# A rebuilt opening: x read feature by token, its squares summed on TensorE, and the gate sums moved out of the dense stream

## The chip, the cores and the metric

The kernel runs on one core of one Trainium2 chip. The metric is device microseconds (us) of one execution; the median of three runs is quoted, and one further execution was taken with the hardware profiler.

## The reference, cut to what matters

One step of a one-layer decoder trunk. There are 1024 prompt tokens and 64 sample tokens (8 sequences of 8), 1088 in all, with 1024 features each. All of it is float32.

```python
shift, scale, gate = jnp.split(jax.nn.silu(c) @ ada_w[l] + ada_b[l], 3, axis=-1)
h = rmsnorm(x, norm_w[l]) * (1.0 + scale[:, None, :]) + shift[:, None, :]
q_lat, kv_lat, k_pe, g_a, u, g_b, m_a, m_b = split_in(h @ w_in[l])   # 4128 columns
...                                   # attention, convolution and recurrence, two output products
x = x + gate[:, None, :] * (merged @ w_out[l])
```

`rmsnorm` divides each token's row by the root of its mean square. The condition `c` has one row for the prompt and one for each of the 8 sample sequences, so `shift`, `scale` and `gate` have 9 rows of 1024.

## The kernel before, in words

**Layout.** Activations stand with features on the 128 partitions and tokens along the free axis, in 8 blocks of features (`k`, 0 to 7). The 1088 tokens are cut into three groups, `GRP`, of 364, 362 and 362; the last ends with the 64 sample tokens. A product is made of three matmuls (`mm3`, L79 to L81): a value is split into a high part that TensorE's fast float32 form takes exactly and a low rest (`split`: ScalarE casts the high part, L55; VectorE subtracts, L56), and high x high, high x low and low x high are summed. Where no split was made, TensorE takes a plain float32 matmul.

**The opening** (L151 to L305). x comes in 9 blocks of 128 tokens, one token to a partition (`x_load`). `x_norm` squares and sums a block on ScalarE (L224), GpSimd forms the inverse root (`rms_pow`, L112 and L113), VectorE or GpSimd scales the block (L229, L227). `x_turn` transposes it on TensorE, 8 transposes a block (L238), and ScalarE or VectorE copies the result from PSUM into `xT` (L239).

Beside that run the sums for shift and scale: `ada_load(k)` fetches 1 MB of weights, `ada_sum` multiplies it with silu(c) on TensorE in 8 plain float32 matmuls of 256 columns, four at a time in four column strips (L194), `ada_turn` transposes the sums (L202) and VectorE forms the 9 shifts and scales of each feature in `aff` (L204 to L206). `h_part` applies them: GpSimd to the prompt's tokens (L245), VectorE to the sample's (L248, L250), and then splits the result into `hh` and `hl`.

Then a loop over `k` multiplies block `k` of h with the first two of 30 column tiles of `w_in` (`u_part`, into 6 PSUM banks): 3 groups x 2 tiles x 3 matmuls = 18 for each `k`, 144 in all. Within block `k`, `ada_turn(k + 1)` and `h_part(k + 1)` are issued behind the first group's matmuls, and `ada_sum` for block `k + 2` behind the second's. At its end ScalarE copies the six banks out (`u_evac`, L145).

**The dense stream** (L308 to L395). The next tiles are multiplied one after another by `project`, 24 triples to a tile, as filler between the steps of the recurrence and of the sample's attention. Beside tiles 2 to 17 runs one `gate_sums` each (L326 to L340): a 256 KB load into the ring of three buffers that the weights use too, 4 plain float32 matmuls of 128 columns in four strips (through `mm`, L65), and a VectorE copy or add of the 128 x 128 result into `sgs` (L336, L338). `sgs` is first used near the kernel's end.

**Order.** TensorE runs in the order of the program. Instructions of the other engines and the DMA issues on SP are ordered by a planner that takes, for an engine that it thinks idle, the earliest instruction of the program that it thinks ready; so work is moved far ahead of its place (the copy of L532 runs at 7.49 us). On the chip each engine then keeps that order. The filler is paced by `clk`, a count of estimated TensorE time.

Of the kernel before, what the change touches and what calls it, by code (L numbers as in the profile page):

```python
# [9 lines left out]
F32 = mybir.dt.float32  # L10
# [33 lines left out]
def trunk_step(ctx: ExitStack, tc: tile.TileContext, a, o):  # L44
# [76 lines left out]
    with ExitStack() as px_:  # L121
# [29 lines left out]
        with ExitStack() as pb, tc.manual_schedule(engines={mybir.EngineType.PE}):  # L151
# [30 lines left out]
            xT = p1.tile([P, KC, N], F32, name="xT", bufs=1)  # L182

            def ada_load(k):
                aw = p1.tile([P, KC, 256], F32, name="aw", bufs=3)
                nc.sync.dma_start(aw, a["ada_ss"][k])
                return aw

            def ada_sum(aw):
# [5 lines left out]
                sa = p1.tile([P, 256], F32, name="sa")  # L195
# [13 lines left out]
            xs = {}  # L209

            def x_load(i):
                n = P if i < 8 else NS
                if i == 6:
                    xs[6] = p1.tile([P, KC, 256], F32, name="aw", bufs=3).rearrange("p a b -> p (a b)")
                    xs[6], xs[7] = xs[6][:, :D], xs[6][:, D:]
                elif i != 7:
                    xs[i] = p1.tile([P, D], F32, name="x", bufs=6)
                nc.sync.dma_start(xs[i][:n], a["xp"][i * P:(i + 1) * P] if i < 8 else a["xs"])

            def x_norm(i):  # L220

                n, x = P if i < 8 else NS, xs[i]
                st = p1.tile([P, 4], F32, name="st", bufs=4)
                S.activation(L[3][:n, :D], x[:n], AF.Square, accum_out=st[:n, 0:1])  # L224
                rms_pow(st[:n, 2:3], st[:n, 0:1], D, st[:n, 1:2])
                if i % 2:
                    G.tensor_scalar(x[:n], x[:n], st[:n, 2:3], 0.0, OP.mult, OP.add)  # L227
                else:
                    V.tensor_scalar(x[:n], x[:n], st[:n, 2:3], None, OP.mult)  # L229

            def x_turn(i):

                n, x = P if i < 8 else NS, xs[i]
                for j in range(2):
                    ps, tag = ((pt, "pt"), (pj, "pj"), (pj, "pj"))[(2 * i + j) % 3]
                    ps = ps.tile([P, 4, P], F32, name="pxt", tag=tag)
                    for k in range(4):
                        T.transpose(ps[:, k, :n], x[:n, (4 * j + k) * P:(4 * j + k + 1) * P], ident[:n, :n])  # L238
                    (S.copy if j == 0 and i % 2 == 0 else V.tensor_copy)(xT[:, 4 * j:4 * j + 4, i * P:i * P + n], ps[:, :, :n])  # L239

            def h_part(k, s, n):

                h = L[2 + k % 2][:, :N]
                m = min(s + n, NP)
                G.tensor_scalar(h[:, s:m], xT[:, k, s:m], aff[:, k, 1, 0:1], aff[:, k, 0, 0:1], OP.mult, OP.add)  # L245
                if s + n > NP:
                    h3 = hs[:, k].rearrange("p (b t) -> p b t", b=NB)
                    V.tensor_tensor(h3, xT[:, k, NP:].rearrange("p (b t) -> p b t", b=NB),  # L248
                                    aff[:, k, 1, 1:9].rearrange("p b -> p b ()").to_broadcast((P, NB, NT)), OP.mult)
                    V.tensor_tensor(h3, h3, aff[:, k, 0, 1:9].rearrange("p b -> p b ()").to_broadcast((P, NB, NT)),  # L250
                                    OP.add)
# [5 lines left out]
            def u_part(k, c, g):  # L257
                s, n = GRP[g]
                if k == 0:
                    pu[c, g] = (pj if g < 2 else pt).tile([P, 512], F32, name=f"pu{c}{g}", tag="pj" if g < 2 else "pt")  # L260
                mm3(pu[c, g][:, :n], [w[:, k, :] for w in u01[c]], [hh[k][:, s:s + n], hl[k][:, s:s + n]],
                    k == 0, k == KC - 1)

            for i in range(8):
                x_load(i)
            for i in range(9):
                x_norm(i)
                x_turn(i)
                if i == 0:
                    x_load(8)  # L270
                if i == 2:
                    aw = ada_load(0)
                if i == 3:
                    u01 = [weights(a["w_in"][c], (0,), (w_u0, None)[c]) for c in range(2)]
                    aw1 = ada_load(1)
                if i == 5:
                    sa = ada_sum(aw)
                if i == 6:
                    ada_turn(0, sa)
            aw = ada_load(2)  # L280
            h_part(0, *GRP[0])
            h_part(0, *GRP[1])
            h_part(0, *GRP[2])
            sa = ada_sum(aw1)
            for k in range(KC):
                if 0 < k and k + 2 < KC:
                    aw = ada_load(k + 2)
# [1131 lines left out]
```

## Time and profile before

| | us |
|---|---|
| median of 3 runs (971.29 to 971.99) | 971.33 |
| the profiled execution | 971.41 |
| its span (first to last instruction) | 969.6 |
| first transpose of x | 9.04 |
| first matmul of `u_part` | 28.32 |
| first matmul of the dense stream | 66.41 |
| first and last group of `gate_sums` | 119.20 and 385.07 |

TensorE is listed as busy for 97% of the span, VectorE 67%, ScalarE 51%, GpSimd 25%; the DMA engines for a third. A matmul's listed duration contains its way through the array: one of 362 columns is listed with 0.33 us, and the next starts 0.167 us after it. So lengths of TensorE's work are taken from start to start.

### The profile page before, as it was taken

To read this page: it belongs to the slowest core of one execution; us is meant where nothing else is said; L and a number is where in the kernel's file an instruction comes from. 1 tells how busy PE (TensorE), PEld (TensorE's weight loads), DVE (VectorE), ACT (ScalarE), POOL (GpSimd) and SP (SyncE) were. 2 spreads that over 40 slices of the span, in tenths; PEclk is the share of its full clock that TensorE was granted. 3 is DMA by queue.
4 is the path that set the end of the run, shared out by engine and by line. 5 is a ranking of instruction groups with operands and counts; after the bars stand their busy time and mean duration, and the time that the engine had idled before them with its cause. 6 is when DMAs were issued, how large, how long until landed. Compare 5 with 4: busy or idle time off the path is not lost. (4 is left out here: it accounts for less than half of the span.)

```text
span 969.6 us, 16493 instructions
## 1 busy us (share of the span) xinstructions
PE 936.1 (97%) x5933; PEld 860.2 (89%) x5933; DVE 645.5 (67%) x1518; ACT 492.2 (51%) x1150; POOL 241.0 (25%) x313
## 2 busy tenths in 40 slices
PE   5899999999999999999999999999999899999997
PEld 4677999999999999999999898888888799998886
DVE  5775664566666777766654367889889785880833
ACT  6447555544445444544443336777687664650311
POOL 5452210332222322222100034444445200000101
PEclk9999999999999999999999999999999999999999
DMA  9843132453443323333422213000011264741421
GB/s 337 287 142 110 49 108 94 146 152 109 141 129 125 113 77 120 103 110 119 117 78 97 65 53 69 12 7 22 7 34 34 69 198 155 246 140 35 152 87 66
DMA packets 52099, 104.62 MB, mean 108 GB/s; under 512 B 8177, under 2 KB 23601, under 8 KB 50994
## 3 DMA queue, kind: packets, MB, share of 16 engines
q1 hardware_dynamic: 46626, 84.69, 26.8%
q0 software_dynamic: 5392, 18.88, 6.6%
q8 instruction: 47, 0.77, 0.3%
q14 instruction: 34, 0.28, 0.1%
HBM read 85.58 MB, written 16.92 MB: 106 GB/s over the span
## 5 line engine op out<-in xcount | busy, mean ns | idle before, releaser
L79 PE MATMUL pj<-hh,whi 128*128 128x362 f32 (+2 forms) x656 | 223.9, 341 | 1.1 <-ACT L L145 1.1
L81 PE MATMUL pj<-hh,wlo 128*128 128x362 f32 (+2 forms) x656 | 217.1, 331 | 0.0
L80 PE MATMUL pj<-hl,whi 128*128 128x362 f32 (+2 forms) x656 | 216.8, 330 | 0.0
L79 PEld LDWEIGHTS pj<-hh,whi 128*128 128x128 f32 x656 | 123.5, 188 | 7.5 <-issue 4.7
L80 PEld LDWEIGHTS pj<-hl,whi 128*128 128x128 f32 x656 | 123.7, 189 | 1.7 <-issue 0.4
L81 PEld LDWEIGHTS pj<-hh,wlo 128*128 128x128 f32 x656 | 123.4, 188 | 1.7 <-issue 0.4
L644 POOL TENSOR_SCALAR nat<-raw 128x1024 fp32r<-128x1024 f32 x32 | 37.0, 1157 | 136.6 <-PE spo L65 81.6
L1038 POOL TENSOR_SCALAR pr<-pr,mx 128x128 f32<-128x128 f32 (+3 forms) x64 | 50.0, 782 | 83.2 <-DVE mx L1037 69.3
L1036 ACT ACTIVATE pr<-pr,mx 128x128 f32<-128x128 f32 (+3 forms) x64 | 49.8, 778 | 12.9 <-DVE mx L1034 12.6
L645 DVE TENSOR_TENSOR nat<-raw,nat 128x1024 fp32r<-128x1024 f32 x32 | 39.0, 1220 | 20.6 <-POOL nat L644 20.6
L641 POOL DMA_INDIRECT raw<-cache_ckv,idx x32 | 33.6, 1049 | 74.9 <-PE ptt L69 44.4
L1052 PE MATMUL ptr<-ident,pr 128*128 128x128 f32 x288 | 45.6, 276 | 4.1 <-DVE ptl L56 2.7
L112 POOL TENSOR_SCALAR ost<-ost 128x1 f32<-128x1 f32 (+1 forms) x9 | 2.9, 324 | 186.0 <-DVE ost L1296 186.0
L1293 ACT ACTIVATE ot<-xo 128x512 f32<-128x512 f32 (+2 forms) x19 | 11.5, 606 | 72.8 <-DVE xo L1292 68.5
L56 DVE TENSOR_TENSOR ptl<-ptr,pth 128x512 fp32r<-128x512 f32 (+1 forms) x80 | 45.7, 577 | 3.6 <-ACT pth L55 2.4
L694 ACT COPY stmp<-pss 64x512 f32<-64x512 f32 (+1 forms) x40 | 19.9, 497 | 55.0 <-PE pss L65 54.7
L56 DVE TENSOR_TENSOR wlo<-wraw,whi 128x512 fp32r<-128x512 f32 x58 | 39.4, 703 | 10.1 <-ACT whi L55 10.0
L55 ACT CAST pth<-ptr 128x512 fp32r<-128x512 f32 (+1 forms) x80 | 39.6, 499 | 9.7 <-PE ptr L1052 9.1
L56 DVE TENSOR_TENSOR tt<-ptt,tt 128x512 fp32r<-128x512 f32 x64 | 41.2, 679 | 4.8 <-ACT tt L55 4.4
L1052 PEld LDWEIGHTS ptr<-ident,pr 128*128 128x128 f32 x288 | 33.0, 140 | 12.6 <-DVE ptl L56 3.9
L55 ACT CAST whi<-wraw 128x512 fp32r<-128x512 f32 x58 | 34.0, 621 | 13.5 <-PE pj L80 13.4
L345 DVE COPY ev<-pj 128x364 f32<-128x364 f32 (+1 forms) x40 | 21.2, 530 | 29.4 <-PE pj L81 28.9
(472 smaller groups left out, 2588.5 us busy)
## 6 DMA issues: line engine op xcount, KB each, us to landing
wraw<-w_in SPq DMA_DIRECT2D x60, 256.0 KB, 3.2
sg<-g_dram SPq DMA_DIRECT2D x16, 544.0 KB, 3.6
aw<-ada_ss SPq DMA_DIRECT2D x8, 1024.0 KB, 7.2
g_dram<-ev SPq DMA_DIRECT2D x40, 181.0 KB, 2.4
wraw<-ada_g SPq DMA_DIRECT2D x16, 256.0 KB, 3.0
oraw<-w_out SPq DMA_DIRECT2D x16, 256.0 KB, 3.2
xo<-xp SPq DMA_DIRECT2D x8, 512.0 KB, 5.3
out_y<-xo SPq DMA_DIRECT2D x16, 256.0 KB, 2.1
```

The source lines that it names most:

```text
L55: S.copy(hi, src)
L56: V.tensor_tensor(lo, src, f(hi), OP.subtract)
L79: T.matmul(out, lhs[0], rhs[0], start=start, stop=False)
L80: T.matmul(out, lhs[0], rhs[1], start=False, stop=False)
L81: T.matmul(out, lhs[1], rhs[0], start=False, stop=stop)
L345: (S.copy if g == 1 else V.tensor_copy)(ev[:, :n], ps[:, :n])
L641: nc.gpsimd.indirect_dma_start(raw.rearrange("p k r -> p (k r)"), None, ckv_rows, bass.IndirectOffsetOnAxis(ap=idx[:, j, b:b + 1], axis=0))
L644: G.tensor_scalar(nat[:, 0], raw, 1.0, 0.0, OP.mult, OP.add)
L645: V.tensor_tensor(nat[:, 1], raw, f(nat[:, 0]), OP.subtract)
L1036: S.activation(pr[:, :w], pr[:, :w], AF.Exp, bias=mx[:, 1:2], scale=-1.0, accum_out=mx[:, 2:3])
L1038: G.tensor_scalar(pr[:, :w], pr[:, :w], mx[:, 3:4], 0.0, OP.mult, OP.add)
L1052: T.transpose(ps[:, k, i, :], pr[i][:, kc * P:(kc + 1) * P], ident)
```

## The change

- The host hands x over feature by token, cut by token group (`xT0` to `xT2`); 6 loads bring it in, and nothing is transposed.
- `x_sum(g)`: for each of 8 feature blocks ScalarE squares 364 (362) tokens, and a plain float32 matmul with a 128 x 128 tile of ones adds them over features. 24 matmuls in all. One row of the result is copied out.
- `x_turn(g)`: three small transposes bring that row onto partitions, `rms_pow` forms the inverse roots on 128 x 3 values.
- `x_spread(g)`: VectorE multiplies the identity by them, three times, and one plain float32 matmul with ones spreads them over all partitions; ScalarE copies the result to `R[g]`.
- `h_part(k, g)` first multiplies x by `R[g]`: VectorE for groups 0 and 1, GpSimd for group 2. Shift and scale of the sample's tokens go from VectorE to GpSimd.
- All three `h_part` calls of a block stay together behind the first group, one block ahead; `aw` has 4 buffers in place of 3.
- The gate sums leave the dense stream. Four `gate_sum` calls of 8 matmuls of 256 columns (the form of `ada_sum`, 1 MB each) stand in the opening: two in the last two blocks, where no `ada_sum` is left, and two behind the last `u_part`.

```diff
-        G.tensor_tensor(out, tmp, nhalf[:n], OP.pow)
+        G.tensor_tensor(out, tmp, nhalf[:n].to_broadcast(tuple(out.shape)), OP.pow)
...
-            xT = p1.tile([P, KC, N], F32, name="xT", bufs=1)
+            xg = [p1.tile([P, KC, n], F32, name=f"xT{g}", bufs=1) for g, (_, n) in enumerate(GRP)]
+            ones = p1.tile([P, P], F32, name="ones", bufs=1)
+            V.memset(ones, 1.0)
...
+            def x_load(g):
                 for j in range(2):
+                    nc.sync.dma_start(xg[g][:, 4 * j:4 * j + 4], a[f"xT{g}"][:, 4 * j:4 * j + 4])
+            def x_sum(g):
+                n = GRP[g][1]
+                ps = pj.tile([P, 512], F32, name="pss_", tag="pj")
+                for k in range(KC):
+                    sq = p1.tile([P, 364], F32, name="sq", bufs=3)
+                    S.activation(sq[:, :n], xg[g][:, k], AF.Square)
+                    T.matmul(ps[:, :n], ones, sq[:, :n], start=k == 0, stop=k == KC - 1)
+                row[g] = p1.tile([P, 364], F32, name="row", bufs=2)
+                S.copy(row[g][0:1, :n], ps[0:1, :n])
+            def x_turn(g):
+                pq = px.tile([P, 4], F32, name="pst", tag="px")
+                for i, m in cut[g]:
+                    T.transpose(pq[:m, i:i + 1], row[g][0:1, i * P:i * P + m], ident[0:1, 0:1])
+                st[g] = p1.tile([P, 8], F32, name="st", bufs=2)
...
+                rms_pow(st[g][:, 4:7], st[g][:, 0:3], D, st[g][:, 0:3])
+            def x_spread(g):
...
+                for i in range(3):
+                    V.tensor_scalar(rinv[:, i], ident, st[g][:, 4 + i:5 + i], None, OP.mult)
+                ps = pt.tile([P, 512], F32, name="prb", tag="pt")
+                T.matmul(ps[:, :n], ones, rinv.rearrange("p i t -> p (i t)")[:, :n], start=True, stop=True)
+                R[g] = p1.tile([P, 364], F32, name=f"R{g}", bufs=1)
+                S.copy(R[g][:, :n], ps[:, :n])
+            def h_part(k, g):
+                x = xg[g][:, k, :n]
+                (V if g < 2 else G).tensor_tensor(x, x, R[g][:, :n], OP.mult)
                 if s + n > NP:
+                    G.tensor_tensor(h3, x3, aff[:, k, 1, 1:9]...to_broadcast((P, NB, NT)), OP.mult)
+                    G.tensor_tensor(h3, h3, aff[:, k, 0, 1:9]...to_broadcast((P, NB, NT)), OP.add)
                     split(hh[k][:, NP:], hl[k][:, NP:], hs[:, k])
+                G.tensor_scalar(h[:, s:m], x[:, :m - s], aff[:, k, 1, 0:1], aff[:, k, 0, 0:1], OP.mult, OP.add)
                 split(hh[k][:, s:m], hl[k][:, s:m], h[:, s:m])
+            def gate_sum(j):
+                ada_sum(aw[KC + j], sgs[:, 256 * j:256 * j + 256])
...
+            x_sum(0)
+            x_turn(0)
+            x_sum(1)
+            x_spread(0)
+            x_turn(1)
+            x_sum(2)
+            x_spread(1)
+            sa = ada_sum(aw[0])
+            x_turn(2)
+            ada_turn(0, sa)
+            h_part(0, 0)
+            h_part(0, 1)
+            x_spread(2)
+            h_part(0, 2)
+            sa = ada_sum(aw[1])
             for k in range(KC):
                 for g in range(3):
+                    u_part(k, g)
                     if k + 1 < KC and g == 0:
                         ada_turn(k + 1, sa)
                         for j in range(3):
+                            h_part(k + 1, j)
+                    if g == 1:
+                        if k + 2 < KC:
+                            sa = ada_sum(aw[k + 2])
+                        elif k + 2 < KC + 2:
+                            gate_sum(k + 2 - KC)
+            gate_sum(2)
+            gate_sum(3)
...
-        def gate_sums(k, q):
...
-                sums = gate_sums(m // 2, m % 2) if 0 <= m < 16 else iter(())
-                next(sums, None)
-                yield
-                next(sums, None)
                 yield
```

## Rows read from the trace of the kernel before

**Rows 1.** The page's first part: busy time, share of span, instructions of TensorE.
```profile
PE 936.1 (97%) x5933; PEld 860.2 (89%) x5933; DVE 645.5 (67%) x1518; ACT 492.2 (51%) x1150; POOL 241.0 (25%) x313
```
**Rows 2.** Windows, 100 us: length, busy of PE, PEld, DVE, ACT, POOL, clock, DMA.
```profile
100.00:200.00 100.00, 98.29 (x627) 93.98 (x626) 56.92 (x91) 54.05 (x88) 20.20 (x20) 1.00 0.32 101
```
**Rows 3.** Waits of TensorE from 66 to 395 us: total, times, longest.
```profile
PE pj L79 <- ACT L L145: 1.1, 1, 1.1
PE pss L65 <- DVE tt L56: 0.8, 1, 0.8
```
**Rows 4.** Timeline of TensorE in the opening: start, length, engine, line, [idle before].
```profile
9.04 6.99 PE L238 MATMUL pxt<-ident,x 128*128 128x128 f32 x32 [9.04 <-DVE x L229]
...
18.16 1.09 PE L238 MATMUL pxt<-ident,x 128*128 128x128 f32 x8 [0.75 <-POOL x L227]
...
28.32 0.43 PE L79 MATMUL pu<-hh,wuh 128*128 128x364 f32 x1 [2.38 <-ACT hh L55]
```
**Rows 5.** Timeline, first 36 us: instructions that a DMA released.
```profile
6.00 1.06 ACT L224 ACTIVATE L<-x 128x1024 f32<-128x1024 f32 x1 [1.30 <-DMA x<-xp]
...
8.74 1.06 ACT L224 ACTIVATE L<-x 128x1024 f32<-128x1024 f32 x1 [0.32 <-DMA x<-xp]
...
19.27 0.59 PEld L194 LDWEIGHTS pada<-aw,sc 128*32 128x32 f32 x16 [0.26 <-DMA aw<-ada_ss]
```
**Rows 6.** Timeline of TensorE, 566 to 577 us: a plain float32 matmul, 512 columns.
```profile
567.93 1.02 PE L938 MATMUL qss<-csr,ones 128*128 128x512 f32 x2
```
**Rows 7.** Windows of 1 us, TensorE: busy, granted clock, DMA share, GB/s.
```profile
29.00:30.00 1.00, 1.00 (x4) 0.52 1.28 336
...
32.00:33.00 1.00, 1.00 (x12) 0.78 0.57 238
```
**Rows 8.** Groups by form, 0 to 66 us: two short instructions, total, mean ns.
```profile
L113 POOL TENSOR_TENSOR st<-st,nhalf 128x1 f32<-128x1 f32 x8 | 4.8, 606 | 0.6
...
L205 DVE TENSOR_SCALAR aff<-ads,vec 128x9 f32<-128x9 f32 x8 | 1.8, 229 | 0.2
```
**Rows 9.** Timeline of TensorE in the loop: around an ada_turn and an ada_sum.
```profile
40.21 0.33 PE L81 MATMUL pu<-hh,wlo 128*128 128x364 f32 x1
...
40.94 0.33 PE L81 MATMUL pu<-hh,wul 128*128 128x362 f32 x1
...
41.43 0.32 PE L81 MATMUL pu<-hh,wlo 128*128 128x362 f32 x1
41.69 1.07 PE L194 MATMUL pada<-aw,sc 128*32 128x256 f32 x16
...
43.13 0.32 PE L81 MATMUL pu<-hh,wul 128*128 128x362 f32 x1
```
**Rows 10.** Timeline of TensorE: a late block of the loop, and the loop's end.
```profile
61.70 0.43 PE L79 MATMUL pu<-hh,wuh 128*128 128x364 f32 x1 [0.20 <-ACT hh L55]
...
66.41 0.43 PE L79 MATMUL pj<-hh,whi 128*128 128x364 f32 x1 [1.06 <-ACT L L145]
```
**Rows 11.** Timeline of TensorE in the dense stream: the first group of gate_sums.
```profile
118.94 0.33 PE L81 MATMUL pj<-hh,wlo 128*128 128x362 f32 x1
119.20 0.42 PE L65 MATMUL pada<-wraw,sc 128*32 128x128 f32 x8
...
119.99 0.33 PE L81 MATMUL pj<-hh,wlo 128*128 128x362 f32 x1
```
**Rows 12.** Groups by form, 36 to 60 us: GpSimd and VectorE in the loop.
```profile
L245 POOL TENSOR_SCALAR L<-xT,aff 128x298 f32<-128x298 f32 x5 | 4.8, 951 | 0.0
...
L245 POOL TENSOR_SCALAR L<-xT,aff 128x362 f32<-128x362 f32 x5 | 3.2, 644 | 0.0
...
L56 DVE TENSOR_TENSOR hl<-L,hh 128x364 fp32r<-128x364 f32 x5 | 2.7, 537 | 4.6 <-ACT hh L55 4.6
```
**Rows 13.** Groups by form, whole span: GpSimd with two inputs.
```profile
L937 POOL TENSOR_TENSOR csr<-csr,sq 128x512 f32<-128x512 f32 x2 | 2.6, 1280 | 64.4 <-ACT sq L908 64.4
```
**Rows 14.** Timeline of VectorE in the loop: two subtractions beside GpSimd.
```profile
42.93 1.39 DVE L56 TENSOR_TENSOR hl<-L,hh 128x364 fp32r<-128x364 f32 x2 [0.91 <-ACT hh L55]
```

More of the change, by code (lines that the diff above doesn't have):

```diff
@@ L207, in ada_turn @@
                                 OP.add, OP.mult)
[L209 to L229, printed above, removed]
@@ L231, in x_turn @@
-            def x_turn(i):
-                n, x = P if i < 8 else NS, xs[i]
-                for j in range(2):
[L235 to L239, printed above, removed]
@@ L241, in h_part @@
-            def h_part(k, s, n):
+            R = {}
+            def x_load(g):
+                for j in range(2):
+                    nc.sync.dma_start(xg[g][:, 4 * j:4 * j + 4], a[f"xT{g}"][:, 4 * j:4 * j + 4])
+            row, st, cut = {}, {}, [[(i, min(P, n - i * P)) for i in range(3)] for _, n in GRP]
+            def x_sum(g):
[7 more added lines that the diff above has]
+                S.copy(row[g][0:1, :n], ps[0:1, :n])
@@ L251, in h_part, with u_part @@
                                     OP.add)
                     split(hh[k][:, NP:], hl[k][:, NP:], hs[:, k])
+                G.tensor_scalar(h[:, s:m], x[:, :m - s], aff[:, k, 1, 0:1], aff[:, k, 0, 0:1], OP.mult, OP.add)
                 split(hh[k][:, s:m], hl[k][:, s:m], h[:, s:m])
+            def gate_sum(j):
+                ada_sum(aw[KC + j], sgs[:, 256 * j:256 * j + 256])
             pu = {}
-            def u_part(k, c, g):
+            def u_part(k, g):
                 s, n = GRP[g]
[L259 to L284, printed above, removed]
-            for k in range(KC):
-                if 0 < k and k + 2 < KC:
-                    aw = ada_load(k + 2)
-                if k == 0:
-                    for c in range(2):
-                        weights(a["w_in"][c], (1,), u01[c])
+                for c in range(2):
+                    if k == 0:
+                        pu[c, g] = (pj if g < 2 else pt).tile([P, 512], F32, name=f"pu{c}{g}",
+                                                             tag="pj" if g < 2 else "pt")
+                    mm3(pu[c, g][:, :n], [w[:, k, :] for w in u01[c]], [hh[k][:, s:s + n], hl[k][:, s:s + n]],
+                        k == 0, k == KC - 1)
@@ new lines, in trunk_step @@
+            for g in range(3):
+                x_load(g)
+            aw = {0: ada_load(0)}
+            u01 = [weights(a["w_in"][c], (0,), (w_u0, None)[c]) for c in range(2)]
+            aw[1] = ada_load(1)
+            for c in range(2):
+                weights(a["w_in"][c], (1,), u01[c])
+            aw[2], aw[3] = ada_load(2), ada_load(3)
+            x_sum(0)
[5 more added lines that the diff above has]
+            x_spread(1)
@@ L293, in trunk_step @@
                 for g in range(3):
-                    for c in range(2):
-                        u_part(k, c, g)
+                    u_part(k, g)
                     if k + 1 < KC and g == 0:
@@ L324, in project @@
                 next(beside, None)
-        def gate_sums(k, q):
-            aw = wp.tile([P, 512], F32, name="wraw", bufs=3)
-            nc.sync.dma_start(aw.rearrange("p (k j) -> p k j", k=4), a["ada_g"][k, :, 4 * q:4 * q + 4])
-            yield
-            ps = pj.tile([P, P], F32, name="pada", tag="pj")
-            for t in range(4):
-                mm(ps[32 * t:32 * t + 32, :], sc[:, 4 * q + t, :], aw[:, P * t:P * t + P], start=True, stop=True)
-            to = sgs[:, P * k:P * k + P]
-            if q == 0:
-                V.tensor_copy(to, ps)
-            else:
-                V.tensor_tensor(to, to, ps, OP.add)
-            if k == 7 and q == 1:
-                nc.sync.dma_start(sgs[9:10], a["gate_b"])
         def spill(c):
@@ L1326, in _layout @@
          "cache_ckv": c(i["cache_ckv"][0]), "cache_kpe": c(i["cache_kpe"][0])}
+    xT = np.concatenate([r["xp"], r["xs"]]).T.reshape(KC, P, N).transpose(1, 0, 2)
+    for g, (s, n) in enumerate(GRP):
+        r[f"xT{g}"] = c(xT[:, :, s:s + n])
     cT = np.zeros((P, KC, 32), np.float32)
```

34 lines of the change are left out of this document (20 added, 14 removed).

## The prediction

> **What bounds the kernel now.** I read the page's busy shares first: TensorE 97%, the next engine 67% [rows 1]. Then the windows: from 100 us on TensorE is busy for 98 of 100 us at granted clock 1.00, which is its 2.4 GHz level [rows 2]. Then TensorE's waits between 66 and 395 us: the longest in total is 1.1 us, the next 0.8 [rows 3]. So in the dense stream whatever TensorE is spared comes off the end. The opening is different. There I read the timeline: transposes begin at 9.04 us, the first matmul of the loop waits until 28.32 [rows 4], and the loop hands over at 66.41 [rows 10]. Before 28.32 the DMA sets the pace (tiles of x release ScalarE at 6.00 and 8.74, the first weights for shift and scale release TensorE at 19.27 [rows 5]), then the copies and the chain through GpSimd and ScalarE. So the change has two accounts: where the dense stream starts, and how much it holds.
>
> **The dense stream: the gate sums go.** Without the group, the matmuls of 362 columns follow each other every 0.167 us: from L81 at 118.94 the third after it would start at 119.44. It starts at 119.99 [rows 11]. So a group costs 0.55 us, though its matmuls are listed with 0.42. There are 16 and TensorE waits for nothing else there [rows 3]: 16 x 0.55 = **-8.8 us**. Their VectorE adds and loads lie beside TensorE, and I count nothing for them.
>
> **The gate sums come back in the opening.** They have the form of `ada_sum`. By the same reckoning L81 after such a sum starts at 43.13 where it would have started at 41.93 [rows 9]: 1.2 us. Four of them: 4.8 us. Two stand behind the last `u_part`, where TensorE now waits 1.1 us for ScalarE to empty the banks [rows 10]. They last 2.4 us, so that wait is covered: -1.2 us with the start of the first matmul. If ScalarE took the copies of the sums first, at most these 1.2 us would come back.
>
> **The start of the loop.** TensorE's program order is now the chain.
> - First matmul. The first two further tiles of x (512 KB each) took from 6.00 to 8.74 [rows 5], 0.38 MB to the us. The first load is 745 KB where it was 524, so it is there 0.55 us later, at 6.55. A square of 1024 columns takes 1.06 us [rows 5]; of 364, about 0.5. Start at 7.2.
> - 24 sums. A plain float32 matmul of 512 columns is two passes, listed with 1.02 us together and 0.594 each; so the second starts 0.43 after the first, and a column costs 0.86/512 us [rows 6]. For 364: 0.61 us; 24 take 14.6. ScalarE makes a square in 0.5, so TensorE sets the pace, and the data (4.46 MB at 0.38 to the us, until about 17) stay ahead.
> - The clock at the start. At the loop's start before, the granted clock was 0.52 from 29 us and 0.78 in the slice from 32 [rows 7], the 1.2 GHz level; matmuls had run since 28.32 [rows 4], so it rose some 4.1 us after they began. The first 32 transposes took 0.22 us each, 8 later ones 0.14 [rows 4]. The rows print 1.00 for both, but I take the first 4.4 us of sums at half speed: +2.2 us. Bounds: 0, if TensorE starts at the upper level, and +4.9, if all of `x_sum(0)` runs at the lower (8 x 0.61).
> - Behind `x_sum(0)` TensorE waits for the copied row (0.5) and turns it (0.3): 0.8. The other two turns: 0.6. Spreads 0 and 1: 1.2. `ada_sum(0)`: 1.2. `ada_turn(0)` with the copy before it: 0.5.
> - `x_spread(2)` waits for the chain of `x_turn(2)`: two VectorE copies, two GpSimd steps, three VectorE products, at 0.23 for a VectorE step and 0.6 for the power [rows 8], with handovers 2.3 us, 0.5 of it beside `ada_turn`. 1.8 us. Behind this waiting matmul stand `ada_sum(1)` and the whole loop, though block 0's first group is long ready. Bounds: 0, if it is hidden, and 1.8 + 1.7, if the clock falls in that gap as it did before 29 us (0.48 + 0.50 + 0.50 + 0.22 us lost in four slices, of which the first and last are shown [rows 7]). Then the spread 0.6 and `ada_sum(1)` 1.2.
>
> Sum: 7.2 + 14.6 + 2.2 + 0.8 + 0.6 + 1.2 + 1.2 + 0.5 + 1.8 + 0.6 + 1.2 = 31.9 us, against 28.32. Bounds 27.9 and 36.3. The transposes, their copies and the scaling of x go, but their place is taken by a chain that is 3.6 us longer.
>
> **The loop.** Before, 66.41 - 28.32 = 38.1 us: 144 matmuls x 0.167 = 24.0; six `ada_sum` (2 to 7) x 1.2 = 7.2; seven `ada_turn` x 0.23 (L81 at 40.94 where 40.71 was due [rows 9]) = 1.6; clock 1.7; the end's wait 1.2; so 2.4 are left for stalls, of which one is seen at 61.70, where h comes late in a block without an `ada_sum` [rows 10]. After: 24.0 + 7.2 + 1.6 + 4.8, the clock up, the end's wait covered. The stall at 61.70 goes, since a gate sum stands there. What is late next is h again, by the multiplication with R. A block's VectorE subtraction takes 0.54 us for 364 columns [rows 12]; the two new products, of the same form, add 1.1 us to VectorE in each block. GpSimd's product of two inputs took 1.28 us for 512 [rows 13], so 0.9 for 362, and the sample's two steps perhaps 0.3 each: 1.5 more beside its three scalings (0.64 alone [rows 12]). A block lasts 18 x 0.167 + 1.2 + 0.23 = 4.4 us and GpSimd would be busy for 3.4 of it. But x times R needs no `aff`: by the planner's rule VectorE does it ahead, while TensorE sums, and the queue behind it is short then. Group 2's product, on GpSimd, can only start when `R[2]` is there, just before the loop, and lies ahead of the scalings that ScalarE and TensorE wait for. I take 2.5 us of stalls, as before. Bounds: 0, and 12, worked out below as a rival. Loop: 24.0 + 7.2 + 1.6 + 4.8 + 2.5 = 40.1.
>
> **Sum.** The dense stream starts at 31.9 + 40.1 = 72.0 in place of 66.4: +5.6. It holds 8.8 us less. Net **-3.2 us**. The profiled execution took 971.41 us (span 969.6 and 1.8 around it), 0.08 above the median, so both give **968.1 us**.
>
> **Rivals.**
> 1. *The opening is quicker than I chain it.* The clock is up by the third sum and the last spread's chain lies beside other work: start at 29.4, one stall less: 964.5. For it: x is there early. Against: nothing stands on TensorE between the last turn and that spread but `ada_turn`.
> 2. *The opening takes all of the gain.* The lower clock lasts through `x_sum(0)` (+2.7) or falls again in the gap (+1.7): 970 to 971, no change. For it: the gap before 28.32 cost just that.
> 3. *VectorE and GpSimd get in each other's way, and the result is slower.* GpSimd's scaling of 298 columns takes 0.95 us, that of 362 only 0.64 [rows 12]; the shorter one runs beside VectorE's subtractions, and these two take 1.39 us together where one alone takes 0.54 [rows 14, 12]. So the engines nearly exclude each other where both have two-input or SBUF-reading work. If the products with R stay inside the loop, a block needs on GpSimd 3 x 0.64 + 0.9 + 0.6 = 3.4 us and on VectorE 1088/364 x 0.54 = 1.6 for the subtractions and 1.1 for the products; one after the other 6.1 us in place of 4.4. Over 7 blocks 12 us of stalls in place of 2.5: 978. It decides from 5.2 us to a block on (2.5 + 3.2 us of stalls over 7 blocks). Against it: the products can run ahead, in an opening in which both engines are mostly idle. The Trainium skill has this as a rule (SBUF — State Buffer, Who interferes with whom): the two engines share a pair of ports as an exclusive lock, and a VectorE instruction with both inputs in SBUF contends with a GpSimd one that reads SBUF. By that rule the full 6.1 would count; the rows agree in kind, with 1.39 us for two subtractions that would take 1.08 alone.
> 4. *The dense stream gives nothing back*, because the paced chains of the sample's attention set its length: +5.6, 977. Against it: 0.8 us is the longest of their waits [rows 3].
>
> **Chances.** Forecast 0.44, rival 1 0.18, rival 2 0.18, rival 3 0.14, rival 4 0.06. What can be told from no change here is 0.2%, or 1.9 us: 969.4 to 973.3. The forecast's case spreads over some 4 us and falls above 969.4 in one case of six; rival 1 is faster, rival 2 mostly the same, rivals 3 and 4 slower but for weak forms of 3. That makes faster 0.56, same 0.25, slower 0.19. The range is 963.5 to 975.0: it takes in rivals 1 and 2 and weak forms of 3, and leaves out the full 978 and 977. The forecast's own range is 966 to 970.5.
>
> **What would show it.** Right: no L65 group `pada` after 75 us; the first `pu` matmul at 30.5 to 33.5; the first `pj` matmul at 70 to 74, with no wait on ScalarE before it; the sums 0.6 us apart after the first few and 1.2 before. Wrong: `pu` before 29 or after 35; blocks of the loop over 5 us, with VectorE or GpSimd waits before `hh` or `hl`; a wait on a load of weights ahead of `ada_sum`; from 120 to 390 us less than 8 us gained.

## The result, and the profile after

The changed kernel takes **988.25 us** (median of 4 runs, 987.71 to 988.42) against 971.43 in the same session (4 runs, 971.29 to 971.99): ratio 1.0164, 95% interval 1.0152 to 1.0176. The forecast was 968.1. The profiled execution has a span of 986.6 us against 969.6: 17.0 us to explain. The page, where [rows 1] had 936.1 us for TensorE:

```profile
PE 948.0 (96%) x5860; PEld 864.5 (88%) x5860; DVE 638.0 (65%) x1503; ACT 494.0 (50%) x1161; POOL 239.8 (24%) x321
```

TensorE has fewer instructions and is busy longer: part of its work ran at the lower clock, and its 24 new sums are plain float32 matmuls, of which eight are listed with 5.13 us at the upper level. Its waits from 5 to 140 us (in total, times, longest) name the places:

```profile
PE pss__191 L228 <- ACT sq L227: 7.0, 1, 7.0
PE prb L251 <- DVE rinv L249: 3.9, 1, 3.9
PE padt L206 <- ACT sa L200: 3.7, 5, 1.1
PE pu L79 <- ACT hh L55: 3.3, 1, 3.3
PE pqt L69 <- DVE kvsq L487: 2.6, 1, 2.6
```

The first is the start, which the forecast had. The other four add up to 13.5 us; before, of these only the loop's first matmul waited over a microsecond, 2.38 us [rows 4]. TensorE's timeline at these places, to be held against [rows 4, 9 and 10]:

```profile
7.02 7.24 PE L228 MATMUL pss__191<-sq,ones 128*128 128x364 f32 x16 [7.02 <-ACT sq L227]
...
21.07 5.45 PE L228 MATMUL pss__273<-sq,ones 128*128 128x362 f32 x16
...
28.06 0.33 PE L236 MATMUL pst<-ident,row 1*128 1x1 f32 x3
...
32.93 1.57 PE L251 MATMUL prb<-rinv,ones 128*128 128x362 f32 x2 [3.87 <-DVE rinv L249]
34.43 1.94 PE L198 MATMUL pada<-aw,sc 128*32 128x256 f32 x16
36.30 0.67 PE L79 MATMUL pu<-hh,wuh 128*128 128x364 f32 x1
...
45.34 0.66 PE L79 MATMUL pu<-hh,wuh 128*128 128x364 f32 x1 [3.35 <-ACT hh L55]
...
59.74 0.44 PE L206 MATMUL padt<-ident,sa 128*128 128x128 f32 x2 [0.79 <-ACT sa L200]
...
84.43 1.93 PE L198 MATMUL pada<-aw,sc 128*32 128x256 f32 x32
86.30 0.44 PE L79 MATMUL pj<-hh,whi 128*128 128x364 f32 x1
...
113.31 0.28 PE L69 MATMUL pqt<-ident,kvsq 64*128 64x64 f32 x1 [2.57 <-DVE kvsq L487]
```

The loop starts at 36.30 instead of 28.32 (+8.0), lasts 50.0 us instead of 38.1 (+11.9), and the sample's queries lose 4.6 more: their last `pqu` matmul is 24.5 us late where the dense stream started 19.9 late. From there to the `pto` matmul at 520.45 us (536.39 after) the lag falls from 24.5 to 15.9: the dense stream gives back 8.6. A late operand at 541 us, with a low clock behind it, costs 1.2. Together 8.0 + 11.9 + 4.6 - 8.6 + 1.2 = 17.1.

Windows of 1 us (busy PE, PEld, DVE, ACT, POOL, clock, DMA share, GB/s) in three of the four stretches in which the granted clock was 0.50, which is the 1.2 GHz level (the other one is at 114 us):

```profile
33.00:34.00 1.00, 1.00 (x2) 0.42 (x2) 1.00 (x2) 0.42 (x2) 1.00 (x2) 0.50 0.95 401
47.00:48.00 1.00, 0.99 (x4) 0.51 (x2) 0.44 (x2) 0.83 (x3) 0.14 (x1) 0.50 0.00 0
...
545.00:546.00 1.00, 1.00 (x4) 1.00 (x4) 0.19 (x1) 0.75 (x3) 0.00 (x0) 0.50 0.00 0
```

They follow the waits for `rinv`, `hh` and `kvsq` and, at 541 us, one of 0.7. By the clock's records they last 6.83, 6.83, 3.41 and 3.41 us, and the matmuls in them lose half of the time that TensorE works there (in the first it still waits for 1.2 us). Before, between the start and the last microseconds, there was one such stretch of 3.41 us, at 29 us [rows 7].

**Why the loop starts late.** VectorE's timeline:

```profile
21.17 0.16 DVE L239 COPY st<-pst 128x2 f32<-128x2 f32 x1 [3.64 <-PE pst L236]
...
24.75 0.53 DVE L262 TENSOR_TENSOR xT<-xT,R 128x364 f32<-128x364 f32 x1
25.20 0.68 DVE L56 TENSOR_TENSOR wlo<-wraw,whi 128x512 fp32r<-128x512 f32 x1
25.80 3.21 DVE L262 TENSOR_TENSOR xT<-xT,R 128x364 f32<-128x364 f32 x7
28.93 0.68 DVE L56 TENSOR_TENSOR wul<-wraw,wuh 128x512 fp32r<-128x512 f32 x1
29.53 0.68 DVE L56 TENSOR_TENSOR wlo<-wraw,whi 128x512 fp32r<-128x512 f32 x1
30.14 0.15 DVE L239 COPY st<-pst 128x2 f32<-128x2 f32 x1
...
31.96 0.91 DVE L249 TENSOR_SCALAR rinv<-ident,st 128x128 f32<-128x128 f32 x3 [0.67 <-POOL st L113]
```

TensorE has turned the third row by 28.4. VectorE copies it at 30.14, since seven products x times R and two weight splits stand ahead in its queue. Nearly all of these products belong to later blocks.

**Why the blocks are long, and the queries late.** GpSimd's timeline:

```profile
38.76 5.37 POOL L262 TENSOR_TENSOR xT<-xT,R 128x362 f32<-128x362 f32 x6
44.12 1.27 POOL L271 TENSOR_SCALAR L<-xT,aff 128x364 f32<-128x364 f32 x2
...
57.58 0.96 POOL L271 TENSOR_SCALAR L<-xT,aff 128x298 f32<-128x298 f32 x1
58.51 0.29 POOL L268 TENSOR_TENSOR hs<-hs,aff 128x64 f32<-128x64 f32 x1
...
109.12 2.57 POOL L574 TENSOR_TENSOR gi<-gi,uc 128x1112 f32<-128x1112 f32 x1 [1.07 <-ACT gi L569]
111.77 0.19 POOL L112 TENSOR_SCALAR kst<-kst 64x1 f32<-64x1 f32 x1
...
112.31 0.56 POOL L113 TENSOR_TENSOR kst<-kst,nhalf 64x1 f32<-64x1 f32 x1
```

Six products of group 2 run ahead of block 1's scalings: TensorE waits 3.35 us. They also run beside VectorE's two steps for block 1's shift and scale:

```profile
41.01 0.68 DVE L209 TENSOR_SCALAR aff<-ads,vec 128x9 f32<-128x9 f32 x1
41.61 0.87 DVE L210 TENSOR_SCALAR aff<-ads,bsc,vec 128x9 f32<-128x9 f32 x1
```

In the later blocks these steps take 0.23 and 0.29 us (the first also in [rows 8]). Shift and scale are there at 42.48 us, and the scalings begin 1.64 us later, at 44.12: both the order of GpSimd's queue and the time that the two engines take from each other are in this wait.

Ahead of the turns in blocks 3 to 6 the sample's shift (L268) comes last on GpSimd, and ScalarE's queue passes the delay on:

```profile
58.83 0.24 ACT L55 CAST hh<-hs 128x64 fp32r<-128x64 f32 x1 [1.33 <-POOL hs L268]
58.98 0.43 ACT L55 CAST hh<-L 128x298 fp32r<-128x298 f32 x1
59.33 0.36 ACT L200 COPY sa<-pada 128x256 f32<-128x256 f32 x1
```

The copy `sa` is what the next `ada_turn` on TensorE (59.74) waits for; TensorE had ended the sum by 56.8. At 109 us it is the recurrence's gi product that runs ahead of the root `kst` of the sample's queries. In the kernel before the root came first:

```profile
86.46 0.19 POOL L112 TENSOR_SCALAR kst<-kst 64x1 f32<-64x1 f32 x1 [0.35 <-ACT kvsq L476]
86.73 0.55 POOL L113 TENSOR_TENSOR kst<-kst,nhalf 64x1 f32<-64x1 f32 x1
87.72 2.58 POOL L565 TENSOR_TENSOR gi<-gi,uc 128x1112 f32<-128x1112 f32 x1 [0.44 <-ACT gi L560]
```

There the first `w_kvq` loads were issued at 62.71, ahead of the dense start (66.41). After, they are issued behind it, and behind the load of the gate bias, which waits for the last gate sum's copy (SP's queue):

```profile
87.39 0.30 SPq L331 DMA_DIRECT2D sgs<-gate_b  x1
87.79 0.37 SPq L546 DMA_DIRECT2D out_conv<-cv  x1
...
88.72 1.33 SPq L461 DMA_DIRECT2D kqr<-w_kvq  x3
```

### The profile page after: what moved, and what is told of

Its sections match the earlier page's. It is cut to its first block, busy times and chain, and to the rows that moved or that the text cites. A ratio compares the mean times of both kernels' runs of the same rounds, so it can differ in the third digit from the quotient of the medians.

```text
span 986.6 us, 16341 instructions
## 1 busy us (share of the span) xinstructions
PE 948.0 (96%) x5860; PEld 864.5 (88%) x5860; DVE 638.0 (65%) x1503; ACT 494.0 (50%) x1161; POOL 239.8 (24%) x321
## 5 line engine op out<-in xcount | busy, mean ns | idle before, releaser
L653 POOL TENSOR_SCALAR nat<-raw 128x1024 fp32r<-128x1024 f32 x32 | 34.4, 1075 | 135.8 <-PE spo L65 66.9
L654 DVE TENSOR_TENSOR nat<-raw,nat 128x1024 fp32r<-128x1024 f32 x32 | 39.1, 1221 | 24.5 <-POOL nat L653 24.4
L650 POOL DMA_INDIRECT raw<-cache_ckv,idx x32 | 31.6, 986 | 75.5 <-PE ptt L69 65.2
L703 ACT COPY stmp<-pss 64x512 f32<-64x512 f32 (+1 forms) x40 | 19.9, 497 | 52.5 <-PE pss L65 52.2
L79 PE MATMUL pout<-woh,mgh 128*128 128x512 f32 (+1 forms) x102 | 38.4, 377 | 0.0
```

What stands on the lines that cost most here:

```text
L79: T.matmul(out, lhs[0], rhs[0], start=start, stop=False)
L650: nc.gpsimd.indirect_dma_start(raw.rearrange("p k r -> p (k r)"), None, ckv_rows, bass.IndirectOffsetOnAxis(ap=idx[:, j, b:b + 1], axis=0))
L653: G.tensor_scalar(nat[:, 0], raw, 1.0, 0.0, OP.mult, OP.add)
L654: V.tensor_tensor(nat[:, 1], raw, f(nat[:, 0]), OP.subtract)
L703: S.copy(tmp[own, :n], ps[other, :n])
```

## The experiments

All ratios are against the kernel before, run on the same chip in turn. First loop matmul, dense start and the eight blocks between them (first `pu` matmul of a block to that of the next), all from TensorE's timelines in the profiled execution. That one was the fastest of its runs in e1 (971.73), e9 (985.28) and e11 (978.91) and the slowest in e2 (994.76) and e6 (993.75); the time is the median of all:

| kernel | first pu | blocks, us | dense start | time, us | ratio (95%) |
|---|---|---|---|---|---|
| before | 28.32 | 6.5 4.6 4.4 4.7 5.2 4.4 3.6 4.7 | 66.41 | 971.43 | |
| after | 36.30 | 9.0 8.1 4.4 5.4 5.4 6.2 5.4 6.1 | 86.30 | 988.25 | 1.0164 (1.0152 to 1.0176) |
| e1_gates_only | 28.40 | 6.1 5.0 4.4 4.7 5.3 4.4 4.4 7.9 | 70.63 | 974.21 | 1.0017 (1.0008 to 1.0027) |
| e2_open_only | 36.78 | 9.0 8.0 4.4 5.4 6.1 5.3 4.5 5.2 | 84.84 | 990.34 | 1.0176 (1.0158 to 1.0194) |
| e3_mul_v | 36.22 | 6.0 6.4 6.3 5.4 5.4 6.2 5.4 6.1 | 83.33 | 986.34 | 1.0156 (1.0128 to 1.0184) |
| e4_h3_v | 36.09 | 8.6 6.1 4.4 4.4 4.4 5.2 4.4 6.1 | 79.86 | 982.84 | 1.0116 (1.0087 to 1.0144) |
| e5_both_v | 36.02 | 5.5 5.6 5.3 5.1 4.4 5.2 4.4 6.1 | 77.66 | 980.80 | 1.0091 (1.0074 to 1.0107) |
| e6_sa_v | 37.96 | 9.9 7.7 4.4 5.9 5.9 4.9 6.8 6.1 | 89.58 | 991.07 | 1.0192 (1.0175 to 1.0209) |
| e9_order | 35.51 | 5.5 5.5 6.1 7.3 6.5 5.7 6.0 6.6 | 84.83 | 988.53 | 1.0174 (1.0157 to 1.0191) |
| e11_order2 | 33.09 | 8.1 5.5 5.6 6.8 5.6 5.6 5.2 6.1 | 81.50 | 979.53 | 1.0089 (1.0070 to 1.0108) |
| e13_order3 | 33.53 | 5.3 6.2 6.2 7.6 6.3 5.1 5.6 6.7 | 82.35 | 981.38 | 1.0096 (1.0079 to 1.0113) |
| e14_no_products | 33.71 | 6.1 5.3 5.3 8.3 6.5 4.4 4.4 6.1 | 80.16 | 981.11 | 1.0077 (1.0055 to 1.0099) |

**The two halves of the change.** e1_gates_only keeps the old opening and moves the gate sums to the loop's end; e2_open_only has the new opening and leaves the gate sums in the dense stream.

```diff
 # e1_gates_only: before, with
+                    elif g == 1:
+                        gate_sum(k + 2 - KC, aw)
+            for j in (2, 3):
+                gate_sum(j, late[j - 2])
+            nc.sync.dma_start(sgs[9:10], a["gate_b"])
...
-                sums = gate_sums(m // 2, m % 2) if 0 <= m < 16 else iter(())
```

> The old opening with the gate sums moved as in the change (two in the last two blocks, two behind the last u_part), three aw buffers as before. If the opening alone is to blame: 16 groups x 0.55 us leave the dense stream (-8.8), four sums of 1.2 come (+4.8), the wait of 1.1 at the loop's end is covered: -5 us, 966 us (964.5 to 967.5). If moving the gate sums is itself a loss (their loads and the gate_b load hold up SP's queue, the sample queries start late as in the changed kernel): 971 to 975.

> The new opening with the gate sums left in the dense stream, where they were. If the two parts are independent: the changed kernel plus 8.8 us in the dense stream, less 4.8 in the loop, plus about 1 us of wait at the loop's end: 993 us (990 to 996). If the gate sums at the loop's end cause the later stall of the sample queries (2.6 us and the low clock behind it): that stall is gone and it is near 988.

The opening alone costs as much as the whole change (1.0176 against 1.0164): dense start 18.4 us late, time within the range for two independent parts. The gate sums alone are no gain either: 974.21 us, in the range of e1's second case. In e1's trace (an execution of 971.73 us; the other nine took 972.27 to 975.47 at a mean clock of 0.991 to 0.993 against 0.995, and what they lose more is in no trace) the dense start is 4.2 us late (1.5 of it a wait of the last sum for its weights), the dense stream gives 8.2 back, and in between the queries lose 4.9: the gi product runs at 93.60 ahead of the root, TensorE waits 2.6 us for `pqt` and its clock is low for 3.41 us behind it.

In e2, where the gate sums stayed, the first `w_kvq` loads go out ahead of the dense start (81.55 us), the root comes ahead of the gi product and the wait for `pqt` is gone. Yet its queries lose 4.7 us too, by another wait, with the clock low for 6.83 us behind it:

```profile
PE pkvq L74 <- DMA kqr<-w_kvq: 2.2, 1, 2.2
```

So the wait for `pqt` belongs to the moved gate sums, but a loss of the same size there comes with the new opening alone as well. Why these later loads are late in e2 I have not tested.

**GpSimd's queue.** e3_mul_v puts group 2's product on VectorE, e4_h3_v the sample's two steps, e5_both_v both.

```diff
-                (V if g < 2 else G).tensor_tensor(x, x, R[g][:, :n], OP.mult)
+                V.tensor_tensor(x, x, R[g][:, :n], OP.mult)         # e3, e5
-                    G.tensor_tensor(h3, x3, ...
-                    G.tensor_tensor(h3, h3, ...
+                    V.tensor_tensor(h3, x3, ...                     # e4, e5
+                    V.tensor_tensor(h3, h3, ...
```

> The changed kernel with group 2's product x times R on VectorE in place of GpSimd. Theory A (order of the queues): GpSimd's six products of later blocks (38.8 to 44.1 us) stood ahead of the scalings of block 1; without them the wait of 3.35 us for hh and the low clock behind it (6.8 us at half) go: 6 to 7 us less, 981 to 982.5; the later blocks stay at 5.4 us. Theory B (the shared ports): VectorE now does the same port work with two inputs, blocks stay long and the total changes by under 2 us: 986 to 988.

> The changed kernel with the sample's shift and scale (two steps on 64 columns) back on VectorE. Theory A: the sample's h is ready early, its cast and the copy of the next ada_sum behind it on ScalarE are no longer late, ada_turn's waits of 0.8 to 1.1 us in each block go: blocks 2 to 7 at 4.5 to 4.8 us, 4 to 6 us less, 982.5 to 984.5; the wait in block 1 stays. Theory B: the steps have two SBUF inputs on either engine, port work is the same, blocks stay over 5.2 us: 987 to 988.

> The changed kernel with the products of group 2 and the sample steps on VectorE, both edits of the two earlier runs together. Queue order (A): block 1 no longer waits behind six products on GpSimd (3.0 us at the dense start alone) and the sum's copy no longer behind the sample cast (6.4 us alone); the two are separate waits, so they add: dense start 77 to 78 us, time 979 to 980. Shared ports or a VectorE that now has too much (B): the two gains overlap, dense start 80 or later, time 982 or more. Both leave the wait of 3.9 us ahead of the third spread and the one in the sample queries.

In e4 the waits of `padt` for `sa` fall from 3.7 us to 0.2 and blocks 2 to 4 take 4.4 us, the length forecast; block 1's wait stays at 3.2, though the clock is low for 3.41 us behind it instead of 6.83. Its time is in theory A's range. In e3 it is the other way round: the waits for `hh` shrink from 3.3 us to 1.6 (0.3 of it ahead of block 1, 1.3 ahead of block 2) and the clock does not fall again there, while `padt` waits 4.9 us. By its time e3 missed: 986.34 us is theory B's range, and the dense start gains 3.0 us where 6 to 7 were written. The products, now on VectorE, run beside GpSimd's scalings of 364 columns, which take 1.74 us (39.87) and 1.23 (46.75) instead of 0.65, and block 2 takes 6.3 us. So e3 removes the order and the shared time in block 1 together, and no run tells their shares apart. The gains at the dense start, 3.0 and 6.4, add up to 8.6 in e5: its dense start is inside the range written down, its time 0.8 us above it. These are two separate waits, both of them a matter of what stands on GpSimd ahead of the late step or beside it. The 3.9 us ahead of the third spread stayed in all three.

**ScalarE's queue.**

```diff
-                S.copy(sa, ps)
+                V.tensor_copy(sa, ps)                               # e6_sa_v
```

> The changed kernel with one edit: the copy of a block's sum (sa) on VectorE instead of ScalarE, the sample steps left on GpSimd. If the five waits of 0.8 to 1.1 us ahead of the turn come from that copy standing behind the casts of hs on ScalarE: they go as in the run with the sample steps on VectorE, dense start 80 to 82.5 us, time 982.5 to 985. If GpSimd's own time for the sample steps makes the blocks long: the waits move to hh and the time stays at 987 to 988.

A miss on both sides (991.07). VectorE's timeline shows why:

```profile
61.26 0.23 DVE L56 TENSOR_TENSOR hl<-hs,hh 128x64 fp32r<-128x64 f32 x1 [1.04 <-ACT hh L55]
61.60 0.47 DVE L56 TENSOR_TENSOR hl<-L,hh 128x298 fp32r<-128x298 f32 x1
61.99 0.42 DVE L200 COPY sa<-pada 128x256 f32<-128x256 f32 x1
```

On VectorE, too, the copy was put behind the sample's work, here its subtraction, which waits for the same late GpSimd step. The wait moved with the copy and did not shrink: in the loop `padt` waits three times, 4.1 us together, in place of four times and 3.45, and once more for 2.2 us ahead of the loop, where the third spread then waits 2.2 instead of 3.9.

**VectorE's queue.** In e9_order, e11_order2 and e13_order3 both of GpSimd's jobs are on VectorE, and in the opening and the loop VectorE and GpSimd issue in the order in which the program is written. The three differ only in that order (e11 and e13 also have gi on VectorE, below).

```diff
-        with ExitStack() as pb, tc.manual_schedule(engines={mybir.EngineType.PE}):
+        with ExitStack() as pb, tc.manual_schedule(engines={mybir.EngineType.PE, mybir.EngineType.DVE, mybir.EngineType.Pool}):
...
 # e9: block 0: scale, products, weight splits, third spread; block k+1: products, turn
 # e11: block 0: scale, third spread, products of blocks 0 and 1; block k+1: turn, products of k+2
 # e13: group 0's products ahead of the third turn; block k+1: turn, scaled rows, then products of k+2
```

> The run before, and in the opening and the loop VectorE and GpSimd issue in the order of the program (written so that the third group's statistics and spread stand ahead of the blocks' scaled rows, and only the products of the coming block stand ahead of its scale and shift). Same instructions, only their order. Queue order (A): the third spread waits under 2.5 us instead of 3.9, the u matmuls start at 32 to 34 us instead of 36.3, block 1 starts without a gap over 1 us, the clock does not fall a second time: dense start 73 to 75 us, time 975 to 977. If the chain from turn to hh is too long for a block of 4.4 us in any order, or ports make it long (B): blocks stay at 5 us and over, dense start 78 or later, time 980 or more.

e9 missed (988.53): its own order was bad. The copies of the third turn came 2.5 us earlier (27.65), but the rows for the spread stood behind products and weight splits, so TensorE still waited 3.7 us.

> The new opening with VectorE and GpSimd in the order of the program as in the run that missed (988.5), but in a better order: the third spread's rows directly behind the scale and shift, products a block earlier behind the scale and shift, the last weight splits behind block 0; the gi product on VectorE. If order alone makes the loop slow (A): the third spread waits under 1.5 us, u matmuls start at 32 to 33.5 us, blocks take 4.4 to 4.7 us, dense start 72 to 75 us; the sample queries lose under 2 us; time 969 to 973. If the chain from turn to hh is too long in any order (B): blocks of 5.2 us and over, dense start 78 or later, time 976 or more.

e11 met the first half: the third spread waits 1.4 us, the loop starts at 33.09, the clock falls once. It missed on the blocks, most of which take 5.5 or 5.6 us. Its groups by form, 38 to 78 us, GpSimd's scaling (total, mean ns):

```profile
L276 POOL TENSOR_SCALAR L<-xT,aff 128x364 f32<-128x364 f32 x7 | 9.8, 1401 | 19.2 <-DVE aff L211 15.5 <-issue 3.7
```

A scaling of 364 columns takes 1.40 us here where [rows 12] has 0.64 for 362, because VectorE's products were put right beside it. In e13 they were not:

```profile
L281 POOL TENSOR_SCALAR L<-xT,aff 128x364 f32<-128x364 f32 x7 | 4.5, 646 | 26.4 <-DVE aff L211 17.6 <-issue 5.4 <-ACT sgs L201 3.4
```

> The run before (979.5: u matmuls from 33.1 us, blocks of 5.5, dense start 81.5) with a third order on VectorE, gi product still there: group 0's products for all blocks in VectorE's idle time ahead of the third turn, the others at the end of a block, so that none runs beside GpSimd's scaling, which took 1.6 to 2.3 us instead of 0.65 beside them. If the shared time of the two engines made those blocks long (ports, with the order deciding what meets): the scaling takes under 0.9 us, blocks 4.4 to 4.8 us, dense start 73 to 76 us, time 971 to 974. If the chain from turn to hh does not fit a block in any order: blocks of 5.2 us and over, dense start 79 or later, 977 or more.

The scaling is back at 0.65 us as forecast, yet the blocks take 6.2. In e9, e11 and e13 time and dense start came out as written for the case that the chain from turn to `hh` does not fit a block; three orders do not show that it fits in none. VectorE's timeline of e13, one turn from reduction to reduction:

```profile
42.88 0.23 DVE L209 TENSOR_REDUCE ads<-padt 128x18 f32<-128x72 f32 x1
...
44.95 1.39 DVE L56 TENSOR_TENSOR hl<-L,hh 128x364 fp32r<-128x364 f32 x2 [1.38 <-ACT hh L55]
...
47.56 0.97 DVE L264 TENSOR_TENSOR xT<-xT,R 128x362 f32<-128x362 f32 x2
48.45 0.68 DVE L56 TENSOR_TENSOR wlo<-wraw,whi 128x512 fp32r<-128x512 f32 x1
49.06 0.22 DVE L209 TENSOR_REDUCE ads<-padt 128x18 f32<-128x72 f32 x1
```

49.06 - 42.88 = 6.18 us, the length of the block: 1.38 of waiting for its own chain through GpSimd and ScalarE, and 4.8 of work. The last run takes work out of that queue: it leaves out the products of groups 1 and 2 in blocks 2 to 7.

```diff
-                        if k + 2 < KC:
-                            x_norm(k + 2)                            # e14_no_products
```

> The third order (981.4) without the products x times R of groups 1 and 2 in blocks 2 to 7 (12 VectorE products left out, so these rows stay unscaled). In that run blocks lasted 6.18 us, and VectorE's turn of one block too, from one reduction of padt to the next: 4.8 us of work and 1.4 us in which it waits for GpSimd's scaling and ScalarE's cast of its own block. If VectorE's queue sets the block: 6.18 - 0.97 = 5.2 us where a weight split (0.68) stands in the block, 4.5 in the others, dense start 75 to 77.5, time 974.5 to 977. If something else does (GpSimd, ScalarE, the loads of weights): blocks stay over 5.6, dense start 79 or later.

VectorE's turns are 5.22 and 5.31 us with a weight split in them, the blocks 5.3, and 4.4 where there is neither: as written for VectorE's queue. The dense start (80.16) is 2.7 us later than expected, since in block 3 two weight casts stand on ScalarE behind the `sa` copy and VectorE waits 2.25 us for them (TensorE 3.25, with a low clock after it). The time, 981.11, missed its range and is no better than e13's: the 2.2 us gained at the dense start are lost again by the queries (1.3) and at 535 us, where the clock is low for 6.83 us instead of 3.41.

**The sample's queries.** e7_old_gi_v is e1 with the gi product on VectorE; e8_old_sp is e1 with nothing that waits ahead of the `w_kvq` loads on SP; e10_old_both has both; e12_after_gi_v is the changed kernel with e7's edit.

```diff
-                    G.tensor_tensor(b, b, uc[:, :NC], OP.mult)
+                    V.tensor_tensor(b, b, uc[:, :NC], OP.mult)      # e7, e10, e12
...
-            nc.sync.dma_start(sgs[9:10], a["gate_b"])               # e8, e10: in dense tile 8 instead
...
-                    nc.sync.dma_start(o["conv"][:, c], cv)
+                    nc.gpsimd.dma_start(o["conv"][:, c], cv)        # e8, e10
```

> The old opening with the gate sums at the loop's end, and the recurrence's gi product (2.6 us on GpSimd, ahead of the sample queries' root there) on VectorE. If that product's place alone makes the gap of 2.9 us ahead of pqt and the low clock behind it (D): the gap falls under 1 us, 969 to 970. If the late w_kvq loads alone do it (C): the gap shrinks at most by half, 972 to 974. VectorE's own queue there is short in the trace (5 to 6 tenths busy), but the product may take as long there.

> The old opening with the gate sums at the loop's end (974.2 us as it was run), but the gate bias is loaded in the middle of the dense tiles and the conv state goes out on GpSimd's queue, so that on SP nothing that waits stands ahead of the first w_kvq loads. SP order (C): these loads are issued by 70 us instead of 72.8, the sample queries are as early against the dense start as in the kernel before, the gap of 2.9 us ahead of pqt and the low clock behind it go: 969 to 970 us, 2 to 3 us under the kernel before. If the loads wait for the loop's memory instead, or GpSimd's gi product stands ahead of the root in any case: the gap stays, 973 to 975.

> The old opening, gate sums at the loop's end, with both repairs of the two runs before at once: nothing that waits ahead of the w_kvq loads on SP, and the gi product on VectorE. Each alone took the wait ahead of pqt away (969.0 and 968.6 us). If it is one and the same wait, both together give 967.5 to 969; if they were two costs, 965 to 966.

> The changed kernel with one edit, the recurrence's gi product on VectorE instead of GpSimd. If that product ahead of the root is what makes PE wait 2.6 us ahead of pqt and lose 1.7 us more at the low clock behind it: 983.5 to 985.5 us, dense start unchanged at 86.3. If that wait is inherited from the late loads: 987 or more.

e7 takes 968.63 us (ratio 0.9967, 0.9954 to 0.9979; 0.4 us under its range), e8 969.04 (0.9968, 0.9954 to 0.9981), e10 968.87 (0.9972, 0.9958 to 0.9985): **all three are some 3 us under the kernel before**, and the two repairs do not add, so they take away the same wait. e8 moves two DMA issues at once, so which of them counts is not shown, and its edit was not tried on the changed kernel. In e8 the loads go out at 70.03 and the root is back ahead of the product:

```profile
92.44 0.18 POOL L112 TENSOR_SCALAR kst<-kst 64x1 f32<-64x1 f32 x1 [0.47 <-ACT kvsq L466]
92.70 0.54 POOL L113 TENSOR_TENSOR kst<-kst,nhalf 64x1 f32<-64x1 f32 x1
93.48 2.59 POOL L555 TENSOR_TENSOR gi<-gi,uc 128x1112 f32<-128x1112 f32 x1 [0.23 <-ACT gi L550]
```

e12 missed by time (986.99; 1.0152, 1.0136 to 1.0167). In the stage itself its trace shows the gain, 3.0 us at the last `pqu` matmul, with the wait for `pqt` down to 0.8. It is lost again at 539 us, where TensorE waits 1.6 us for an operand instead of 0.7 and the clock is low for 6.83 us instead of 3.41. Why that operand is later there I have not tested.

## Why the prediction was wrong, point by point

- **The dense stream**: right. Forecast -8.8; it gave back 8.6 here and 8.2 in e1.
- **The first matmul, the sums, the cold start**: right. First sum at 7.02 for 7.2; the first 8 sums took 7.24 us and the next 8 5.13, so 2.1 for the clock, where 2.2 was taken; the third sum ended at 26.4.
- **`x_spread(2)` waits 1.8 us**: the step that failed first. It waited 3.9, and the clock fell, so that the loop started at 36.30, the upper bound. The sentence that was wrong is "by the planner's rule VectorE does it ahead, while TensorE sums, and the queue behind it is short then". VectorE did do the products ahead, but the rows of R come late (ScalarE has copied the first at 21.5 us, the second at 27.6), so products, most of them for later blocks (seven from 25.80 to 29.01), and the weight splits fell into the very microseconds in which the third row's statistics had to pass. The row stood for 1.75 us in the queue; from its copy to the spread it then took 2.8, where 2.3 was forecast. In e11, with the rows for the spread put ahead, the copy came as soon as the row was turned, the same chain took 2.2, the wait was 1.4 us and the loop started at 33.09; 1.2 of the 4.4 us missing remain.
- **"I take 2.5 us of stalls, as before"**: wrong by some 10 us. Block 1's wait of 3.35 and the four of `padt` in the loop (3.45; the fifth, 0.23, is ahead of it) come from what stands on GpSimd ahead of the late step or beside it, as e3, e4 and e5 show; most of the rest is the low clock in the loop, some 4.5 us (half of 2.25 from 36.30 and of 6.83 from 45.38). I had priced the sample's two steps (0.3 each; they took 0.66 and 0.29) as time on GpSimd, not as the last thing that ScalarE's `sa` copy stands behind. The product of group 2 I had as lying "just before the loop, ahead of the scalings", and gave it no time of its own, though six at 0.9 us stand there.
- **The end's wait**: right. No wait on ScalarE at 86.30; the two gate sums ahead of it took 1.87 us, where 2.4 was taken.
- **"Their VectorE adds and loads lie beside TensorE, and I count nothing for them"**: this failed for what was moved. In e1 the gate bias's load, which waits for the last sum, went ahead of the queries' loads on SP, and the order on GpSimd turned round; that cost the whole gain of the move, as e7, e8 and e10 show. Here the queries lose 4.6 us. The same order on GpSimd has a part in it, since e12 has them 3.0 us earlier; but e2 loses 4.7 there without the move, so the loss cannot be put down to the move alone.
- **Rival 3** (ports) forecast 978 from products that stay inside the loop. VectorE's did not stay there, and in blocks 2 to 7 GpSimd's scaling of 362 columns took 0.65 us, as before. But its mechanism has a share that was not measured apart: VectorE's steps for block 1 took 0.68 and 0.87 us beside GpSimd's products instead of 0.23 and 0.29, and the sample's product on GpSimd 0.66 in the later blocks instead of 0.29 (45.36). In e11 it shows as 1.40 us for 0.65. The Trainium skill (SBUF — State Buffer, Who interferes with whom) says that the two engines' shared pair of ports is an exclusive lock and that issue order decides who blocks; e11 against e13, the same instructions in another order, agrees (1.40 and 0.65 us).
- That a late instruction delays ready ones behind it has a rule too: the Trainium skill (PSUM — Partial Sum Buffer, Engine vs sequencer instructions) calls the queues of ScalarE, VectorE and GpSimd strictly first in, first out. The waits above agree: the row turned by 28.4, the sum ended by 56.8 and the squares ready at 109.4 us stood behind other work on VectorE, ScalarE and GpSimd.

Counted up, forecast against trace: loop start +3.6 and +8.0, loop +2.0 and +11.9, queries 0 and +4.6, dense stream -8.8 and -8.6, the operand at 541 us 0 and +1.2.

What stays open is whether the new opening can be had without loss. The orders tried have either an early start (33.1 us in e11) or short blocks (4.4 us in four of e4's eight), not both: the products are 24 x 0.46 = 11 us of VectorE, and either they run ahead of the chain or they lengthen VectorE's turn of a block (e13, e14). An order that meets both, or the products on another engine, was not tried. Open, too, are the shares of order and shared time in block 1's wait, and the queries' loss in e2.

## What to carry over

Where a planner orders the queues, work that is ready early is not free: look up at what time it becomes ready, and which chain passes through that engine's queue then. Price a step moved to another engine by its place in that queue and by what stands behind its consumer on the next one, not by its length alone. When a block of work moves, follow its small DMAs as well: in e1 a bias load that waits and a store behind it stood ahead of the next stage's loads, and with both out of the way (e8) the order of that stage, which was never touched itself, turned back.

## What the hardware showed that I had not expected

- After one gap of 3.9 us on TensorE (29.0 to 32.9) the clock was at its lower level for 6.83 us, and again for 6.83 after the gap ahead of block 1 (42.0 to 45.3): a wait of 3.35 us cost 3.4 more. Between the two it was back at 1.00 for 6.8 us. The length of a wait did not tell this price: behind waits of 1.4 us ahead of the third spread the clock was low for 6.83 us in e11, for 3.41 in e13, and in e14 it did not fall.
- GpSimd's scaling of 364 columns: 0.65 us alone, 1.40 on average in e11, beside VectorE's products of two inputs. The other way round, beside GpSimd's products, VectorE's two steps on 9 columns took 0.68 and 0.87 us instead of 0.23 and 0.29.
